# Seven half-size products in the place of eight: an MLP's first matrix product by one level of Strassen's scheme

## The chip, the cores and the metric

One core of a Trainium2 chip runs the kernel. Its engines work side by side: TensorE (PE; PEld is its loading of weights), VectorE (DVE), ScalarE (ACT), GpSimd (POOL) and SyncE (SP), which issues the transfers. The metric is device time of one execution in microseconds (us), as a median of several.

## The reference

The model is four layers deep: two hybrid attention layers, then two more layers, each with an attention mixer, an MLP and a small gated addition. There are 512 tokens and 1024 features. The part that is changed is the MLP of the last two layers:

```
hn = rms(h, g_mlp_pre[i])
y = jnp.square(jax.nn.relu(hn @ w_mlp_in[i])) @ w_mlp_out[i]
h = h + rms(y, g_mlp_post[i])
```

`w_mlp_in` is 1024 x 4096 and `w_mlp_out` is 4096 x 1024, all in float32.

## The kernel before

Everything is kept transposed: features on the 128 partitions, the 512 tokens along the free dimension. A 1024-feature activation is therefore eight tiles of 128 x 512 ("kc").

**Precision.** Each float32 operand is split in two tiles of the type fp32r: `h`, the value cast by ACT, and `l`, the rest, found by a subtraction on DVE or POOL. A product is then three matmuls: `wh` by `xh`, `wh` by `xl`, `wl` by `xh`.

**Weights.** `wload` (L370) brings a chunk of weights in pieces of 128 x 512 (256 KB). For each piece SP issues a transfer into a `wraw` buffer (a ring of four), ACT casts it into a `wh` tile (ring of three, L384), and DVE or POOL in the rotation DVE, POOL, DVE subtracts into a `wl` tile (ring of three, L386). I call that a cut. `proj` (L392) makes the matmuls of one chunk into one PSUM bank.

**MLP.** `mlp` (L1339) goes twice through a half of the 4096 hidden features. For each of the half's 16 chunks `fc` it runs `proj` over the eight activation tiles (24 matmuls of 512 columns), takes the maximum with zero on DVE (L1350), squares on POOL (L1351), casts on ACT (L1354) and subtracts on DVE (L1355); the results `fh`, `fl` stand in a ring of 16. Then, for each of the eight output tiles `oc`, it runs `proj` over the 16 hidden tiles (48 matmuls) and copies or adds the bank to `y`. The squared normalisation factor `r2` is multiplied in behind that, so the first product runs on activations that are scaled by the gain alone.

**Around it.** `tail_layer` (L1391) first calls `post`, which normalises the mixer's output, adds it to `h` and splits `h` into the activation tiles one kc after the other; the order of these DVE instructions is written out by hand. The weights of the first four chunks (AHEAD) are cut before, into `fh`/`fl` tiles. `ple_load` brings a small operand `p` for the gated addition, and from the third `oc` of the second half on the weights of the gate are brought ahead. PSUM has six banks for matmuls here. Otherwise a planner that works from estimated costs fixes each engine's order when the kernel is built; on the chip every engine runs its list strictly in that order.

Of the kernel before, what the change touches and what calls it, by code (L numbers as in the profile page):

```python
# [33 lines left out]
AHEAD = 4  # L34
# [254 lines left out]
class Kern:  # L289
# [178 lines left out]
    def halves(s, T):  # L468
        return [(0, T)] if T <= 512 else [(0, T // 2), (T // 2, T // 2)]
# [862 lines left out]
    def ple_proj(s, weights):  # L1332
        for w in weights:
            (ps, _, _), = s.proj(w, s.pa, [(0, NX)])
            t = s.t512("s", 16)
            s.nc.scalar.activation(t, ps, AF.Copy, scale=0.5)
            s.pp.append(t)

    def mlp(s, l, acts, rstd, fp, w, ahead):  # L1339
        nc = s.nc  # L1340
        ys = []
        acc = s.new_acc()
        r2 = s.tp.tile([P, NT], F32, tag="rstd", bufs=2, name=s.nm("r2"))
# [47 lines left out]
    def tail_layer(s, l, ys, acc):  # L1391

        with ExitStack() as ps:
            s.rings(ps, **RINGT)
            s.pp = []
            pw = s.ple_weights(l, range(0, PLE1))
            with s.tc.tile_pool(name=f"ff{l}", bufs=16) as fp, s.tc.tile_pool(name=f"pe{l}", bufs=1) as pep:

                w, wg = [], []

                def ftiles():
                    return [fp.tile([P, NX], F32R, tag=x, name=s.nm(x)) for x in ("fh", "fl")]
# [4 lines left out]
                s.ple_load(l, lambda: pep.tile([P, NX], F32R, name=s.nm("p")))  # L1407


                ys, acc = s.mlp(l, acts, rstd, fp, w, lambda oc: wg.append(s.wload(s.a[f"wpg{l}"][oc], s.xtiles)))  # L1410
# [433 lines left out]
```

## Time and profile before

| what | us |
|---|---|
| median of 3 runs (2803.01 to 2809.76) | 2805.97 |
| profiled execution | 2807.34 |
| its span, first to last instruction | 2805.6 |
| first MLP, from its steady part to its last matmul | about 1655 to 1989 |
| second MLP | about 2412 to 2745 |

The profiled execution takes 1.74 us more than its span. The two MLPs are nearly a quarter of the span.

### The profile page before, as it was taken

The page shows a single profiled execution, that of the slowest core. Times are in us where ns is not written, and L with a number is a line of the kernel's source. Part 1 is how long each engine was busy: PE and PEld are TensorE (multiplying, and loading weights), DVE is VectorE, ACT ScalarE, POOL GpSimd, SP SyncE. Part 2 cuts the span into 40 slices and gives each one's busy share as a digit, 9 for nine tenths or more (in the row PEclk, how much of TensorE's full clock was granted, in tenths as well). Part 3 has the DMA queues.
Part 4 walks back from the last instruction along what each step waited for, and adds up shares of the span by engine and source line. Part 5 has one row for each costly group of instructions (what it writes and reads, how often), then busy time and mean ns, then how long its engine had stood idle before and what let it go on. Part 6 is the DMA issues. An engine that isn't in the chain of part 4 may idle for free.

```text
span 2805.6 us, 41607 instructions
## 1 busy us (share of the span) xinstructions
PE 2717.9 (97%) x15114; PEld 2330.4 (83%) x15122; DVE 1601.9 (57%) x2977; ACT 1233.1 (44%) x2275; POOL 1134.6 (40%) x1064
## 2 busy tenths in 40 slices
PE   8999999999999999999999999999998899999999
PEld 8999999999889887887777778888776777888887
DVE  5666667644576666545667763133549776622335
ACT  5545444433454444344456642233334665322332
POOL 3455345432334344345555442134316433422341
PEclk9999999999999999999999999999989999999999
DMA  4222232234322223335422223324223202233341
GB/s 147 66 69 77 76 104 80 80 99 137 100 71 74 71 88 94 99 91 181 115 79 82 73 83 95 96 93 126 76 65 90 72 28 73 77 94 94 95 126 58
DMA packets 145518, 252.09 MB, mean 90 GB/s; under 512 B 19552, under 2 KB 30688, under 8 KB 145312
## 3 DMA queue, kind: packets, MB, share of 16 engines
q1 hardware_dynamic: 145312, 249.43, 29.4%
q8 instruction: 119, 1.95, 0.3%
q14 instruction: 87, 0.71, 0.1%
HBM read 215.26 MB, written 6.42 MB: 79 GB/s over the span
## 4 chain that ended last, share of the span: by engine, by line
PE 85%; DVE 8%; ACT 3%; issue 2%; POOL 1%; DMA 1%; SPq 0%; POOLq 0%; DVEq 0%; ACTq 0%
PE mm L363 70%; PE st L363 5%; PE pv L363 5%; PE ssq L419 2%; PE sm L363 1%; DVE zr L702 1%; DVE sm L515 1%; DVE sc L1790 1%; DVE m L1789 1%; DVE wl L386 0%; PE rb L454 0%; DVE sc L1707 0%; DVE h L1295 0%; PE vt L794 0%; DVE Pl L565 0%
## 5 line engine op out<-in xcount | busy, mean ns | idle before, releaser
L384 ACT CAST wh<-wr 128x512 fp32r<-128x512 f32 (+2 forms) x734 | 442.9, 605 | 933.6 <-PE mm L363 781.7
L363 PE MATMUL mm<-xh,wh 128*128 128x264 f32 (+1 forms) x2328 | 793.4, 342 | 21.1 <-ACT xh L1153 7.6
L363 PE MATMUL mm<-xl,wh 128*128 128x264 f32 (+1 forms) x2344 | 796.7, 341 | 1.8 <-DVE xl L1154 1.8
L363 PE MATMUL mm<-xh,wl 128*128 128x264 f32 (+1 forms) x2328 | 788.8, 340 | 0.6 <-DVE wl L386 0.5
L386 POOL TENSOR_TENSOR wl<-wr,wh 128x512 fp32r<-128x512 f32 (+2 forms) x257 | 329.5, 1282 | 794.7 <-ACT wh L384 786.1
L386 DVE TENSOR_TENSOR wl<-wr,wh 128x512 fp32r<-128x512 f32 (+2 forms) x477 | 364.9, 766 | 370.3 <-ACT wh L384 361.8
L363 PEld LDWEIGHTS mm<-xh,wh 128*128 128x128 f32 x2328 | 440.1, 189 | 74.1 <-issue 8.5
L363 PEld LDWEIGHTS mm<-xl,wh 128*128 128x128 f32 x2344 | 444.3, 190 | 52.0 <-DVE xl L1154 3.1
L363 PEld LDWEIGHTS mm<-xh,wl 128*128 128x128 f32 x2328 | 439.5, 189 | 50.3 <-issue 1.2
L565 POOL TENSOR_TENSOR Pl<-P,Ph 128x512 fp32r<-128x512 f32 (+4 forms) x108 | 130.6, 1209 | 185.2 <-ACT P L564 174.2
L363 PE MATMUL mm<-fh,wl 128*128 128x512 f32 x512 | 202.3, 395 | 0.0
L363 PE MATMUL mm<-fl,wh 128*128 128x512 f32 x512 | 202.0, 395 | 0.0
L363 PE MATMUL mm<-fh,wh 128*128 128x512 f32 x512 | 202.0, 395 | 0.0
L564 ACT ACTIVATE Ph<-st 128x512 fp32r<-128x512 f32 (+4 forms) x224 | 122.1, 545 | 142.5 <-PE st L363 84.9
L565 DVE TENSOR_TENSOR Pl<-P,Ph 128x512 fp32r<-128x512 f32 (+4 forms) x108 | 83.7, 775 | 117.7 <-ACT P L564 102.6
L363 PE MATMUL mm<-c,wh 128*128 128x264 f32 (+2 forms) x480 | 128.9, 355 | 10.6 <-ACT q L1724 4.8
L702 DVE RECIPROCAL zr<-zr 128x128 f32<-128x128 f32 (+1 forms) x144 | 123.2, 916 | 4.0 <-ACT zr L711 3.6
L1351 POOL TENSOR_TENSOR ff<-ff 128x512 f32<-128x512 f32 x64 | 81.6, 1274 | 100.2 <-DVE ff L1350 100.0
L564 ACT ACTIVATE P<-st 128x512 f32<-128x512 f32 (+4 forms) x216 | 116.7, 540 | 4.7 <-POOL Pl L565 2.3
L363 PEld LDWEIGHTS mm<-fl,wh 128*128 128x128 f32 x512 | 96.5, 188 | 22.5
L363 PEld LDWEIGHTS mm<-fh,wl 128*128 128x128 f32 x512 | 96.5, 188 | 22.4
L363 PEld LDWEIGHTS mm<-fh,wh 128*128 128x128 f32 x512 | 96.5, 188 | 22.3
(631 smaller groups left out, 5425.2 us busy)
## 6 DMA issues: line engine op xcount, KB each, us to landing
wr<-in_win_dram SPq DMA_DIRECT2D x240, 256.0 KB
wr<-in_wmi_dram SPq DMA_DIRECT2D x128, 256.0 KB
wr<-in_wmo_dram SPq DMA_DIRECT2D x128, 256.0 KB
wr<-in_wbr_dram SPq DMA_DIRECT2D x48, 256.0 KB
wr<-in_wab_dram SPq DMA_DIRECT2D x48, 256.0 KB
wr<-in_wout_dram SPq DMA_DIRECT2D x32, 256.0 KB
wr<-in_wpg_dram SPq DMA_DIRECT2D x32, 256.0 KB
wr<-in_wuq_dram SPq DMA_DIRECT2D x32, 192.0 KB
```

The costliest lines, as they stand in the source:

```text
L363: s.last_mm = s.nc.tensor.matmul(out, l, r, start=start, stop=stop)
L384: nc.scalar.copy(h, raw)
L386: s.weng[s.wn % len(s.weng)].tensor_sub(l, raw, h.bitcast(F32))
L419: s.summed = s.nc.tensor.matmul(ps[:m, b:b + 1], a[:, P * b:P * b + m], s.ones[:, 0:1], start=first and b == 0, stop=last and b == bs[-1])
L515: nc.vector.tensor_tensor_reduce(out=ps[:, col:col + nk], in0=ps[:, col:col + nk], in1=mk, scale=-1.0, scalar=init, op0=OP.add, op1=OP.min ...
L564: nc.scalar.activation(o[:, :col], ps[:, :col], AF.Exp)
L565: s.pl_eng(ui, hn).tensor_sub(pl[:, :col], p[:, :col], ph[:, :col].bitcast(F32))
L702: s.nc.vector.reciprocal(t[:, a:b], t[:, a:b])
L1351: nc.gpsimd.tensor_mul(f, f, f)
L1789: nc.vector.max(m8, score[b][:, :n])
L1790: nc.vector.match_replace(out=score[b][:, :n], in_to_replace=m8, in_values=score[b][:, :n], imm_value=-3e38)
```

## The change

The first product of the MLP is made for pairs of chunks. With the features in halves (kc 0 to 3 and 4 to 7) and the tokens in halves of 256, a pair of 128-feature output chunks is a 2 x 2 block product; Strassen's scheme (in Winograd's form) makes it with seven block products in the place of eight. Four sums of the weights (`S1` to `S4`) and four sums of the activations replace some operands. The activation sums are made once for each layer by `quarters`; the weight sums are made for each pair in `mlp_pair`. The first four chunks of each layer stay as they were, so there are 14 pairs in each layer.

The second product runs in four parts of eight hidden tiles, and the ring of `fh`/`fl` tiles holds one part. `ple_load` moves into the fourth part. Four tiles (`s.spare`, called `e`) are temporaries of `quarters`, then buffers of `mlp_pair`, and at last tiles of `ple_proj`.

```diff
+    def quarters(s, l, acts, sp, e):
...
+        for j in range(KC // 2):
+            x, y, u, v = e
+            for t, kc in ((x, j), (y, KC // 2 + j)):
+                nc.scalar.activation(t, s.h[kc], AF.Copy, scale=s.gcol(f"fpre{l}", kc))
+            nc.vector.tensor_sub(u[:, :H], x[:, H:], x[:, :H])
+            nc.vector.tensor_sub(u[:, H:], y[:, H:], u[:, :H])
+            nc.vector.tensor_sub(v[:, :H], y[:, H:], x[:, H:])
+            nc.vector.tensor_sub(v[:, H:], y[:, :H], u[:, H:])
+            h, lo = (sp.tile([P, 2 * NX], F32R, tag=t, bufs=4, name=s.nm(t)) for t in ("th", "tl"))
+            for i, t in enumerate((u, v)):
+                r = slice(NX * i, NX * i + NX)
+                nc.scalar.copy(h[:, r], t)
+                nc.vector.tensor_sub(lo[:, r], t, h[:, r].bitcast(F32))
...
+    def mlp_pair(s, l, p, q, e, fp, sp):
...
+        def cut(raw, pool, tags, eng):
+            h, lo = (pool.tile([P, NX], F32R, tag=t, bufs=3, name=s.nm(t)) if pool is sp else
+                     pool.tile([P, 4, P], F32R, tag=t, bufs=3, name=s.nm(t)).rearrange("p m n -> p (m n)") for t in tags)
+            nc.scalar.copy(h, raw)
+            eng.tensor_sub(lo, raw, h.bitcast(F32))
+            return h, lo
...
+        a11 = load(2 * p, 0)
+        a21 = load(2 * p + 1, 0, e[2 + odd])
+        a22 = load(2 * p + 1, 4)
+        a12 = load(2 * p, 4)
+        w11 = cut(a11, s.wp, W, V)
+        G.tensor_add(e[0], a21, a22)
+        w12 = cut(a12, s.wp, W, G if odd else V)
+        G.tensor_sub(e[1], e[0], a11)
+        s2 = cut(e[1], sp, S, V)
+        G.tensor_sub(a21, a11, a21)
+        s1 = cut(e[0], sp, S, G)
+        G.tensor_sub(a12, a12, e[1])
+        s3 = cut(a21, sp, S, V)
+        w22 = cut(a22, s.wp, W, G)
+        s4 = cut(a12, sp, S, V)
...
+        prod(b1, 0, w11, q[0], True, True)
+        nc.scalar.copy(t[:, :H], b1[:, :H])
+        prod(b2, 1, w12, q[1], True, False)
+        prod(b2, 0, s2, q[5], False, True)
+        u2 = t[:, H:NX]
+        V.tensor_add(u2, t[:, :H], b2[:, :H])
+        V.tensor_add(g[:, :H], t[:, :H], b2[:, H:])
+        prod(b3, 0, s1, q[4], True, False)
+        prod(b3, 1, s3, q[6], False, True)
...
+        V.tensor_tensor(two(v), u2.unsqueeze(1).to_broadcast([P, 2, H]), two(b3), op=OP.add)
+        V.tensor_add(g[:, 3 * H:], v[:, H:], b3[:, :H])
+        prod(b4, 1, w22, q[3], True, False)
+        prod(b4, 0, s4, q[2], False, True)
+        V.tensor_add(g[:, H:3 * H], v, b4)
+        V.scalar_tensor_tensor(g, g, 0.0, g, op0=OP.max, op1=OP.mult)
...
+        nc.scalar.copy(fh, g)
+        V.tensor_sub(fl, g, fh.bitcast(F32))
...
-        for half in range(2):
+        for part in range(4):
...
+            for p in range(4 * part + len(ff) // 2, 4 * part + 4):
+                ff += s.mlp_pair(l, p, q, s.spare, fp, sp)
             for oc in range(KC):
-                if half == 1 and oc in range(2, 2 + AHEAD):
+                if part == 3 and oc in range(2, 2 + AHEAD):
                     ahead(oc - 2)
-                (ps, _, _), = s.proj(s.wload(s.a[f"wmo{l}"][oc, :, 16 * half:16 * half + 16]), ff, [(0, NX)])
+                (ps, _, _), = s.proj(s.wload(s.a[f"wmo{l}"][oc, :, 8 * part:8 * part + 8]), ff, [(0, NX)])
...
```

Each `prod` is 12 matmuls of 256 columns. `V` is DVE and `G` is POOL.

## Rows read from the trace of the kernel before

**Rows 1.** The page: busy us (share of the span) and instructions of TensorE.
```profile
PE 2717.9 (97%) x15114; PEld 2330.4 (83%) x15122; DVE 1601.9 (57%) x2977; ACT 1233.1 (44%) x2275; POOL 1134.6 (40%) x1064
```

**Rows 2.** Stretches of the first MLP: length, busy us by engine, granted clock, DMA.
```profile
1655.00:1719.00 64.00, 64.00 (x277) 51.72 (x276) 27.63 (x40) 21.84 (x37) 26.61 (x22) 1.00 0.29 91
1719.00:1815.00 96.00, 96.00 (x415) 77.82 (x414) 17.37 (x26) 25.66 (x44) 15.67 (x12) 1.00 0.31 95
1815.00:1909.00 94.00, 94.00 (x407) 75.93 (x405) 35.41 (x54) 29.92 (x51) 35.76 (x29) 1.00 0.29 94
1909.00:1990.00 81.00, 80.63 (x356) 65.64 (x354) 24.82 (x33) 25.37 (x42) 33.07 (x24) 1.00 0.38 120
```

**Rows 3.** The chain that ended last, whole span: start us, us, what.
```profile
566.58 105.49 PE mm L363 x864
...
1620.40 3.40 DMA wr<-in_wmi_dram
...
1655.10 319.36 PE mm L363 x1374
...
2411.96 320.88 PE mm L363 x1386
```

**Rows 4.** DVE in order of time, the MLP's seventh and eighth chunk: start us, us, instruction.
```profile
1670.02 0.69 DVE L1350 TENSOR_SCALAR ff<-mm 128x512 f32<-128x512 f32 x1 [1.08 <-PE mm L363]
1675.60 0.69 DVE L1350 TENSOR_SCALAR ff<-mm 128x512 f32<-128x512 f32 x1 [2.01 <-PE mm L363]
```

**Rows 5.** TensorE in order of time, near the end of the span.
```profile
2795.06 0.39 PE L363 MATMUL mm<-fh,fl 128*128 128x512 f32 x1
2795.29 0.28 PE L363 MATMUL mm<-fh,fh 128*128 128x256 f32 x1
...
2800.92 0.28 PE L363 MATMUL mm<-fh,fl 128*128 128x256 f32 x1
```

**Rows 6.** Groups of instructions by line and shape, 1655 to 1719 us.
```profile
L1351 POOL TENSOR_TENSOR ff<-ff 128x512 f32<-128x512 f32 x13 | 16.4, 1264 | 19.0 <-DVE ff L1350 19.0
L384 ACT CAST wh<-wr 128x512 fp32r<-128x512 f32 x23 | 14.3, 620 | 28.3 <-PE mm L363 22.2 <-issue 6.1
L386 DVE TENSOR_TENSOR wl<-wr,wh 128x512 fp32r<-128x512 f32 x15 | 11.0, 738 | 10.1 <-ACT wh L384 10.1
L386 POOL TENSOR_TENSOR wl<-wr,wh 128x512 fp32r<-128x512 f32 x8 | 10.4, 1296 | 17.8 <-ACT wh L384 17.8
L1355 DVE TENSOR_TENSOR fl<-ff,fh 128x512 fp32r<-128x512 f32 x13 | 9.8, 755 | 13.3 <-ACT fh L1354 13.2
L1350 DVE TENSOR_SCALAR ff<-mm 128x512 f32<-128x512 f32 x12 | 8.3, 689 | 13.6 <-PE mm L363 13.5
```

**Rows 7.** DVE in order of time, in the stretch before the first MLP.
```profile
1629.61 0.74 DVE L1292 SCALAR_TENSOR_TENSOR xh<-xh,gain,rb 128x512 f32<-128x512 f32 x1
1630.26 1.62 DVE L386 TENSOR_TENSOR wl<-wr,wh 128x512 fp32r<-128x512 f32 x1
1631.80 1.78 DVE L1263 SCALAR_TENSOR_TENSOR xl<-h,gain,xh 128x512 fp32r<-128x512 f32 x1
1633.50 0.68 DVE L1295 TENSOR_TENSOR h<-h,xh 128x512 f32<-128x512 f32 x1
...
1644.79 1.62 DVE L1263 SCALAR_TENSOR_TENSOR xl<-h,gain,xh 128x512 fp32r<-128x512 f32 x2
```

**Rows 8.** POOL in order of time, the same stretch.
```profile
1630.03 2.99 POOL L484 TENSOR_TENSOR acc<-acc,sq 128x512 f32<-128x512 f32 x2 [2.10 <-issue]
```

**Rows 9.** The chain's last pieces, on 256-column operands: start us, us, what.
```profile
2801.24 0.39 ACT th L1383
...
2801.65 0.44 DVE th L1384
...
2802.11 0.42 DVE h L1385
```

**Rows 10.** TensorE in order of time: the last matmul of the four prepared chunks.
```profile
1656.33 0.39 PE L363 MATMUL mm<-xh,fl 128*128 128x512 f32 x1
```

More of the change, by code (lines that the diff above doesn't have):

```diff
@@ L1334, in ple_proj @@
             (ps, _, _), = s.proj(w, s.pa, [(0, NX)])
-            t = s.t512("s", 16)
+            t = s.spare.pop(0) if s.spare else s.t512("s", 16)
             s.nc.scalar.activation(t, ps, AF.Copy, scale=0.5)
             s.pp.append(t)
-    def mlp(s, l, acts, rstd, fp, w, ahead):
+    def quarters(s, l, acts, sp, e):
         nc = s.nc
-        ys = []
+        H = NX // 2
+        q = [[] for _ in range(7)]
+        for j in range(KC // 2):
[11 more added lines that the diff above has]
+                nc.vector.tensor_sub(lo[:, r], t, h[:, r].bitcast(F32))
+            for k, (c, r) in enumerate(((j, slice(0, H)), (KC // 2 + j, slice(0, H)), (KC // 2 + j, slice(H, NX)))):
+                q[k].append((acts[c][0][:, r], acts[c][1][:, r]))
+            for k, i in ((4, 0), (5, 1), (6, 2), (3, 3)):
+                r = slice(H * i, H * i + H)
+                q[k].append((h[:, r], lo[:, r]))
+        return q
@@ new lines, in mlp_pair, with load, prod @@
+    def mlp_pair(s, l, p, q, e, fp, sp):
+        nc = s.nc
+        H = NX // 2
+        src = s.a[f"wmi{l}"]
+        s.wn += 1
+        odd = s.wn % 2
+        def load(ch, k0, t=None):
+            t = s.wp.tile([P, 4, P], F32, tag="wraw", bufs=4, name=s.nm("wr")) if t is None else \
+                t.rearrange("p (m n) -> p m n", m=4)
+            nc.sync.dma_start(t, src[ch, :, k0:k0 + 4])
+            return t.rearrange("p m n -> p (m n)")
+        def cut(raw, pool, tags, eng):
[4 more added lines that the diff above has]
+            return h, lo
+        W, S = ("wh", "wl"), ("sh", "sl")
+        V, G = nc.vector, nc.gpsimd
+        a11 = load(2 * p, 0)
[13 more added lines that the diff above has]
+        s4 = cut(a12, sp, S, V)
+        b1, b2, b3, b4 = (s.bank("mm", "mm") for _ in range(4))
+        def prod(ps, c, w, xs, first, last):
+            o = ps[:, H * c:H * c + H]
+            for j, (xh, xl) in enumerate(xs):
+                r = slice(P * j, P * j + P)
+                s.mm(o, w[0][:, r], xh, first and j == 0, False)
+                s.mm(o, w[0][:, r], xl, False, False)
+                s.mm(o, w[1][:, r], xh, False, last and j == 3)
+        t, v = s.tmp("t"), s.tmp("v")[:, :NX]
+        g = sp.tile([P, 2 * NX], F32, tag="g", name=s.nm("g"))
+        prod(b1, 0, w11, q[0], True, True)
[7 more added lines that the diff above has]
+        prod(b3, 1, s3, q[6], False, True)
+        two = lambda x: x.rearrange("p (b c) -> p b c", b=2)
+        V.tensor_tensor(two(v), u2.unsqueeze(1).to_broadcast([P, 2, H]), two(b3), op=OP.add)
[4 more added lines that the diff above has]
+        V.scalar_tensor_tensor(g, g, 0.0, g, op0=OP.max, op1=OP.mult)
+        fh, fl = (fp.tile([P, 2 * NX], F32R, tag=x, name=s.nm(x)) for x in ("fh", "fl"))
+        nc.scalar.copy(fh, g)
+        V.tensor_sub(fl, g, fh.bitcast(F32))
+        return [(fh[:, :NX], fl[:, :NX]), (fh[:, NX:], fl[:, NX:])]
@@ L1342, in mlp @@
+    def mlp(s, l, acts, rstd, fp, sp, w, tiles, ahead):
+        nc = s.nc
         acc = s.new_acc()
@@ L1344, in mlp @@
         nc.gpsimd.tensor_mul(r2[:, :NX], rstd[:, :NX], rstd[:, :NX])
-        for half in range(2):
+        ys = [s.t512("s", 16) for _ in range(KC)]
+        s.spare = [s.t512("s", 16) for _ in range(4)]
+        q = s.quarters(l, acts, sp, s.spare)
+        for part in range(4):
             ff = []
-            for fc in range(16):
-                (ps, _, _), = s.proj(w.pop(0) if w else s.wload(s.a[f"wmi{l}"][16 * half + fc]), acts, [(0, NX)])
+            for fc in range(len(w)):
+                (ps, _, _), = s.proj(w.pop(0), acts, [(0, NX)])
                 f = s.tmp("ff")[:, :NX]
@@ L1351, in mlp @@
                 nc.gpsimd.tensor_mul(f, f, f)
-                fh = fp.tile([P, NX], F32R, tag="fh", name=s.nm("fh"))
-                fl = fp.tile([P, NX], F32R, tag="fl", name=s.nm("fl"))
+                fh, fl = tiles()
                 nc.scalar.copy(fh, f)
@@ L1394, in tail_layer, with halves, get, ahead @@
             s.rings(ps, **RINGT)
-            s.pp = []
+            s.pp, s.spare = [], []
             pw = s.ple_weights(l, range(0, PLE1))
-            with s.tc.tile_pool(name=f"ff{l}", bufs=16) as fp, s.tc.tile_pool(name=f"pe{l}", bufs=1) as pep:
+            with s.tc.tile_pool(name=f"ff{l}", bufs=4) as fp, s.tc.tile_pool(name=f"st{l}", bufs=1) as sp:
                 w, wg = [], []
-                def ftiles():
-                    return [fp.tile([P, NX], F32R, tag=x, name=s.nm(x)) for x in ("fh", "fl")]
+                def halves(pool, tags):
+                    left = []
+                    def get():
+                        if not left:
+                            a, b = (pool.tile([P, 2 * NX], F32R, tag=x, bufs=4, name=s.nm(x)) for x in tags)
+                            left.extend([(a[:, :NX], b[:, :NX]), (a[:, NX:], b[:, NX:])])
+                        return left.pop(0)
+                    return get
+                ftiles, stiles = halves(fp, ("fh", "fl")), halves(sp, ("th", "tl"))
+                def ahead(oc):
+                    if oc == 0:
+                        pt = [x for _ in range(2) for x in stiles()]
+                        s.ple_load(l, lambda: pt.pop(0))
+                    wg.append(s.wload(s.a[f"wpg{l}"][oc], s.xtiles))
                 acts, acc = s.post(ys, acc, f"mpost{l}", f"fpre{l}", pw, lambda: w.extend(
@@ L1406, in tail_layer @@
                 rstd = s.rstd_of(acc, NX, 1024)
[L1407 to L1410 removed]
+                ys, acc = s.mlp(l, acts, rstd, fp, sp, w, ftiles, ahead)
                 pw = s.ple_weights(l, range(PLE1, 4))
```

13 lines of the change are left out of this document (6 added, 7 removed).

## The prediction, made before the changed kernel had run

> **What bounds the kernel now.** I read the page's first table first: TensorE is busy for 97% of the span [rows 1]. That share could hide slack, so I looked at the MLP by stretches: from 1655 to 1990 us TensorE has next to no idle time, while in the two stretches that hold the first product, 158 us together, DVE and POOL each have some 95 us of room [rows 2]. The chain of waits says the same more sharply. One unbroken piece of matmuls is 319.36 us long in the first MLP and 320.88 us in the second [rows 3]. So today a microsecond taken from TensorE there is a microsecond of the kernel, as long as nobody else becomes late.
>
> The pace: the seventh and the eighth chunk are evicted 5.58 us apart [rows 4], and a chunk is 24 matmuls, so a 512-column matmul costs 232.5 ns. I take this and not the chain's 319.36/1374, because a few matmul records may be missing.
>
> **What the products save.** A pair of chunks costs 2 x 5.58 = 11.16 us. After the change it is 7 x 12 = 84 matmuls of 256 columns. What is one worth? The trace has 48 of them: the first starts at 2795.29, the last at 2800.92, which is 5.63/47 = 120 ns each, while the 512-column one just before takes 0.23 us [rows 5]. That stretch is quiet; but 864 matmuls of 264 columns in a loaded stretch take 105.49 us, 122.1 ns each [rows 3], so load hardly costs narrow matmuls anything. I take 120 ns: 10.08 us a pair, 1.08 us saved, 30 us over 28 pairs. Bounds: half of 232.5 (116 ns, 39 us saved) and 120 plus the 5 ns by which 512 columns are slower in the MLP than in the quiet stretch (125 ns, 18 us saved).
>
> The Trainium skill ("TensorE: Matmul & The Clock Gate", Back-to-back issue gap) gives 262 cycles for 256 columns, which at its 2.4 GHz is 109 ns, and 518 cycles, 216 ns, for 512. By that the saving would be 33 us as an estimate; the rows show 120 and 232.5 ns, and they decide.
>
> **What the weight sums cost.** Before, a pair needs four cuts and two evictions. Now it needs seven cuts (ACT 0.62 us each), four sums on POOL, and on POOL also the low parts of s1, w22 and, in every other pair, w12: 6.5 POOL instructions of 1.30 us, 8.4 us [rows 6]. DVE makes 4.5 low parts, five additions from PSUM (three of 256 columns, two of 512, some 2.6 us by 0.42 and 0.69 us [rows 6, 9]) and two instructions over 1024 columns, which no row shows. From 0.42 us for 256 and 0.69 for 512 columns I estimate 1.2 us each. Alone, each of the two engines fits into 10.08 us.
>
> They are not alone. In the stretch before the MLP, DVE's subtraction at 1630.26 takes 1.62 us in the place of 0.68, and the next instruction 1.78 [rows 7], and POOL's two additions, begun at 1630.03, take 2.99 us and not 2.6 [rows 8]. The ends fit a strict turn: DVE finishes at 1631.88 and 1633.58, one POOL instruction apart. The DVE instruction at 1629.61, which takes one operand from PSUM, ran beside POOL at its usual 0.74 us [rows 7]. So a DVE instruction with two SBUF operands and a POOL instruction exclude each other, and one of each costs 1.70 us together (1633.58 - 1631.88). In the MLP as it is, this is rare: the subtractions there average 738 and 755 ns [rows 6].
>
> A pair now has 6.5 POOL instructions and 6.5 such DVE instructions, two of them twice as wide (0.55 us for the other 512 columns, from (0.69 - 0.42)/256 x 512): 6.5 x 1.70 + 2 x 0.55 = 12.15 us, more than TensorE's 10.08. The second product pays back: in its 96 us [rows 2] DVE and POOL are nearly idle. What counts is how much of the sums is done ahead. The rings for `sh`/`sl` and `wh`/`wl` hold three, so about one pair can be. In a part with four pairs TensorE needs 40.3 us, and the last cut must stand 1.44 us before its end, at 38.9. Until then this shared access must carry the rest of the first pair (w22 1.3, s4 0.55, two wide ones at 1.1: 4.0 us), two pairs less the two sums made ahead (24.3 - 2.6), the fourth without its wide ones (10.0), and two cuts for the second product (two thirds on DVE: 0.8 each): 37.3 us. With no gap it just fits. But both engines run in order, behind ACT's casts and ring places that matmuls free; I take nine tenths as used, so 41.4 us and 2.5 us of TensorE waiting. Bounds: none, and 7.7 us at eight tenths.
>
> **End of a part.** The second product now needs its seventh hidden tile after 18 matmuls, 4.2 us. From the last product of a pair that tile takes 0.69 (addition), 1.2, some 1.1 on ACT (from 0.39 and 0.62 us [rows 6, 9]) and 1.2: 4.2 us and the hand-overs. I take 0.5 us of wait; bounds 0 and 1.5.
>
> A full part: -4.32 + 2.5 + 0.5 = -1.3 us; there are six: -7.9 us.
>
> **Opening of the MLP.** The temporaries of `quarters` are the very tiles into which a21 is loaded and the first two weight sums are written. So the first pair's sums can't begin before `quarters` ends. The activations are complete at 1646.4 [rows 7]. DVE then owes the normalisation's 1.1 us and four times (four subtractions over 256 columns, 0.42 us, two over 512, 0.69): 12.2 us. Then the load of a21 (3.40 us in the chain [rows 3]), two sums on POOL (2.6), a cast and a subtraction (1.3), 0.3 for hand-overs: S2's product starts at 1667.3. TensorE's four direct chunks end at 1656.6 [rows 10]; until then it used to make a few matmuls of the next two chunks between them, and w11 and w12 (2.9 us) can take their place. w22 (1.4) fills a little more. So TensorE waits some 9 us. Four products (5.8) and a pair (10.1) end at 1683.1; with 1.5 us of the waits above, 1684.6. Before, the eighth chunk ended at 1675.6 [rows 4]. That is 9.0 us lost in each layer, 18 in both. Bounds: 2 each if half of `quarters` slips in among DVE's earlier work (6 us earlier) and the chain is a microsecond shorter, 17 each if DVE's other work comes first.
>
> **Small parts.** Sixteen more additions of `y` in each layer (0.69 us) read PSUM, so neither POOL nor TensorE waits; if DVE were full they would add 11 us of its time. The weights of the second product are the same bytes in the same pieces. In the fourth part the gate's weights and `p` come in 45 us in the place of 90, four pieces in 5.58 us through four `wraw` buffers, where one load takes 3.40 us [rows 3]: 0.5 us in each layer, 1 in all, up to 4 each. POOL's squares and DVE's maxima of 28 pairs go; they were hidden.
>
> **Sum.** -7.9 + 18 + 1 = +11.1 us on the profiled 2807.34, so 2818.4; that execution is 1.4 us above the median of 2805.97, so 2817, 0.4% slower. A measurement of this kernel tells about 0.2% (5.6 us) from no change.
>
> **Rivals.** (1) *Not slower: the shared access never holds TensorE up.* For: 37.3 us fit before 38.9, and the order may put sums ahead while the second product runs. Against: hardly any room is left. Each full part gives 0.5 - 4.32 = -3.8 us, and 6 x -3.8 + 19 = -3.9: 2802; with an opening of 6 us, 2796. Not slower begins at a use of about 0.92. Chance 0.25: 0.13 within 0.2%, 0.12 faster.
>
> (2) *A short opening.* For: DVE waits for POOL's turns before 1646 [rows 7], gaps an order made from estimates may mean to fill. Against: DVE runs there back to back. At 2 us in each layer, -7.9 + 4 + 1 = -2.9: 2803; without the waits in the parts, 2787. Chance 0.20: 0.13 faster, 0.07 within.
>
> (3) *The shared access sets the pace.* For: 12.15 against 10.08 us a pair, and the turn-taking in [rows 7, 8]. Against: little of it in the MLP so far [rows 6]. At a use of 0.85 TensorE waits 5.0 us in a part: 6 x 1.2 + 19 = +26, 2832; at 0.8, 2848. Chance 0.19, slower. The Trainium skill ("GPSIMD Engine Reference", Key points) has this as a rule: POOL shares its SBUF interfaces with VectorE and contends with DVE instructions that read two SBUF inputs. By that rule the trace agrees, with 1.78 us for a 0.7 us instruction.
>
> (4) *A long opening.* The direct chunks' eight DVE instructions (5.5 us) and POOL's turns come ahead of `quarters`: 8 us more in each layer, 2833. Chance 0.07, slower.
>
> (5) *Narrow matmuls don't save*, at 125 ns: 2817 + 12 = 2829. Against: [rows 5] and the 122.1 ns. Chance 0.03, slower.
>
> **How the numbers follow.** The forecast has 0.26: 0.22 slower, 0.04 within 0.2%; its own range is 2809 to 2826. Faster: 0.12 + 0.13 = 0.25. Same: 0.13 + 0.07 + 0.04 = 0.24. Slower: 0.22 + 0.19 + 0.07 + 0.03 = 0.51. The range from 2788 to 2840 takes in rivals 1 and 2 down to their low ends, and rival 3 to a use of 0.83.
>
> **What would show it.** Right: matmuls of 256 columns at 120 ns; DVE subtractions and POOL instructions in the pairs well above 0.69 and 1.30 us; TensorE idle for some 9 us before S2's first product, with the load of a21 behind `quarters`, and for 2 to 3 us in each four pairs, waiting for `sl`, `wl` or POOL's sums; second products at 5.58 us for 24 matmuls. Wrong: pairs following each other at 10.1 us to the end of a part (rival 1), or at 12 and more from the second on (rival 3); no gap in the opening (rival 2); a first product of the fourth pair that waits for a transfer; or a granted clock below 1.00 inside the MLP, which I have not priced.

## The result and the profile after

The changed kernel takes 2854.57 us (median of four, 2852.99 to 2858.71) against 2806.83 for the kernel before (2803.01 to 2809.76): a ratio of 1.0178, 95% interval 1.0166 to 1.019. It is 48 us slower, where 11 were forecast, and lies outside the stated range of 2788 to 2840. The profiled execution has a span of 2852.8 us, 47.2 more than before.

The page's first line answers to [rows 1]:

```profile
PE 2707.2 (95%) x16122; PEld 2371.0 (83%) x16130; DVE 1841.4 (65%) x3193; ACT 1301.6 (46%) x2391; POOL 1316.6 (46%) x1152
```

TensorE has 10.7 us less work than before, DVE 239 us and POOL 182 us more, and TensorE's share of the span falls. To see where, I cut both MLPs at the same events: from the first of the norm's 40 small matmuls (line 419) to the last eviction of each part (the instruction that copies or adds an output bank to `y`; the expectations count the parts from 0). Before, a part is a quarter of the MLP: the first ends eight chunks' pitch behind the eighth chunk [rows 4], 1675.60 + 8 x 5.58 - 1609.89 = 110.3 us, a middle one takes 16 x 5.58 = 89.2, and the last is what remains.

| us, first / second MLP | forecast, each | before | after | change |
|---|---|---|---|---|
| opening and part 1 | +9.0 | 110.3 / 109.7 | 129.0 / 128.1 | +18.7 / +18.4 |
| part 2 | -1.3 | 89.2 / 88.6 | 89.0 / 89.5 | -0.2 / +0.9 |
| part 3 | -1.3 | 89.2 / 88.6 | 88.5 / 90.9 | -0.7 / +2.3 |
| part 4 | -0.8 | 90.3 / 90.1 | 95.1 / 95.9 | +4.8 / +5.8 |

That is +50 us in the MLPs. The rest of the kernel has the same code, yet its order came out differently (+3.8 us up to the first norm, -8.1 between the MLPs, +1.7 behind them): together some 2.7 us less, which I don't explain.

**The stretches** of the first MLP answer to [rows 2] (length, busy us of PE, PEld, DVE, ACT, POOL, granted clock, DMA):

```profile
1650.00:1680.00 30.00, 14.95 (x67) 11.62 (x66) 23.96 (x36) 13.72 (x25) 12.98 (x11) 0.74 0.10 32
...
1702.00:1745.00 43.00, 43.00 (x198) 35.16 (x197) 12.35 (x14) 15.76 (x28) 14.24 (x11) 1.00 0.30 93
1745.00:1794.00 49.00, 45.33 (x346) 43.06 (x345) 42.60 (x46) 19.65 (x33) 35.39 (x21) 1.00 0.31 97
...
1833.00:1883.00 50.00, 47.03 (x358) 44.69 (x357) 42.40 (x46) 20.89 (x35) 37.65 (x23) 1.00 0.31 95
```

Three things are to be seen: TensorE half idle in the opening, at a lower clock; no idle time in a second product (1702 to 1745); and 3.0 to 3.7 us of it in each four pairs, with DVE busy for 42.6 of 49 us and POOL for 35.4. Much of these two shares is waiting inside an instruction, as the rows of the pairs below show.

In the second MLP the granted clock is below 1.00 inside the pairs too. These are the pairs of its third and fourth part, and TensorE behind a wait in the third:

```profile
2603.00:2652.00 49.00, 44.96 (x348) 43.79 (x348) 41.71 (x45) 19.33 (x34) 36.78 (x22) 0.97 0.29 92
2693.70:2740.00 46.30, 42.77 (x327) 42.09 (x327) 39.44 (x43) 19.35 (x34) 35.05 (x21) 0.93 0.26 81
```

```profile
2623.50 0.47 PE L363 MATMUL mm<-xh,sl 128*128 128x256 f32 x1 [1.94 <-DVE sl L1383]
2623.77 0.42 PE L363 MATMUL mm<-xh,sh 128*128 128x256 f32 x1
2623.98 0.42 PE L363 MATMUL mm<-xl,sh 128*128 128x256 f32 x1
```

Five such runs of 14 to 16 matmuls, 0.21 us apart and not 0.12, stand behind waits of 1.3 to 2.1 us in the pairs: one in the first MLP (fourth part), four in the second (one each in the second and third part, two in the fourth). They cost some 1.4 us each, 7 us in all. Not every wait of that length has one: the 2.14 us before 1775.25 and 1863.76 have none.

**The opening in TensorE's time.** TensorE in order of time, around its one long gap:

```profile
1662.17 1.02 PE L454 MATMUL rb<-rstd,ones 128*128 128x512 f32 x2
1677.73 0.58 PE L363 MATMUL mm<-th,sh 128*128 128x256 f32 x1 [14.54 <-ACT sh L1382]
...
1681.20 0.41 PE L363 MATMUL mm<-th,wl 128*128 128x256 f32 x1
1681.41 0.36 PE L363 MATMUL mm<-xh,wh 128*128 128x256 f32 x1
1681.61 0.28 PE L363 MATMUL mm<-xl,wh 128*128 128x256 f32 x1
1681.72 0.28 PE L363 MATMUL mm<-xh,wl 128*128 128x256 f32 x1
```

S2's product starts after 14.54 us of nothing, 64.1 us after the norm's sums begin (63.9 in the second MLP, with 14.52 us); the forecast had it at 57.4 and the wait at 9. Behind the gap most of the narrow matmuls stand 0.21 to 0.22 us apart, from 1681.6 on 0.12. So the first seventeen ran at the lower of the clock's two levels (1.2 GHz; the granted clock is 0.54 from 1677 to 1682 and 1.00 in the 4 us behind): 3.88 us in the place of 17 x 0.12, 1.8 us lost.

What TensorE waited for is in the chain of waits:

```profile
1670.10 0.60 DVE fl L1454
1670.70 0.61 DVE tl L1357
1671.38 2.92 DMA s<-in_wmi_dram
1674.44 1.25 POOL s L1393
1675.78 1.27 POOL s L1395
1677.06 0.63 ACT sh L1382
1677.73 13.34 PE mm L363 x95
```

The last subtraction of `quarters` (L1357), the load of a21 into the tile that this sets free, two sums, a cast. That is the predicted chain, and from the load on it takes 6.35 us (7.6 forecast). The error is ahead of it: `quarters` ends at 1671.3, 57.7 us after the norm's sums begin, and not 49.8 us after them (1659.7 by the times of the kernel before). DVE in order of time, in the stretch that answers to [rows 7]:

```profile
1645.45 0.41 DVE L1350 TENSOR_TENSOR s<-s,s 128x256 f32<-128x256 f32 x1
1645.78 1.51 DVE L1351 TENSOR_TENSOR s<-s,s 128x256 f32<-128x256 f32 x1
1647.22 0.68 DVE L1295 TENSOR_TENSOR h<-h,xh 128x512 f32<-128x512 f32 x1
...
1654.32 0.74 DVE L1263 SCALAR_TENSOR_TENSOR xl<-h,gain,xh 128x512 fp32r<-128x512 f32 x1
```

And the stretch around it, with the columns of the stretches above:

```profile
1636.00:1656.00 20.00, 19.21 (x92) 15.32 (x91) 20.00 (x27) 11.17 (x19) 9.73 (x7) 0.96 0.00 0
```

DVE has no free moment. The subtractions of `quarters` (L1349 to L1357) stand between the activation tiles, and one of 256 columns that meets POOL takes 1.51 us and not 0.41. So the last activation tile is ready at 1655.06, 41.4 us after the norm's sums begin, where it was 36.5 (1646.4 - 1609.9), and `quarters` goes on among the maxima and subtractions of the direct chunks until 1671.3.

**A pair.** DVE in the second part: the squared maximum (L1430) and the last subtraction (L1433) of a pair are the two instructions over 1024 columns.

```profile
1754.64 2.31 DVE L1430 SCALAR_TENSOR_TENSOR g<-g 128x1024 f32<-128x1024 f32 x1
1756.87 1.78 DVE L1383 TENSOR_TENSOR wl<-wr,wh 128x512 fp32r<-128x512 f32 x1
1758.58 2.31 DVE L1433 TENSOR_TENSOR fl<-g,fh 128x1024 fp32r<-128x1024 f32 x1
1760.81 0.41 DVE L1420 TENSOR_TENSOR t<-t,mm 128x256 f32<-128x256 f32 x1
...
1767.26 2.31 DVE L1430 SCALAR_TENSOR_TENSOR g<-g 128x1024 f32<-128x1024 f32 x1
...
1780.38 2.32 DVE L1430 SCALAR_TENSOR_TENSOR g<-g 128x1024 f32<-128x1024 f32 x1
...
1788.84 1.23 DVE L1430 SCALAR_TENSOR_TENSOR g<-g 128x1024 f32<-128x1024 f32 x1
```

What is uncontended at 1.23 us takes 2.31, and 512 columns take 1.78, while the addition that reads PSUM (L1420) keeps its 0.41. The squared maxima of three pairs stand 12.6 and 13.1 us apart, the last 8.5 us behind the third, when POOL makes one low part of a weight (at 1785.9) and no more sums. The shared access was forecast at 12.15 us a pair.

**The end of the MLP.** DVE's last eviction in the first MLP, before, with its wait for the last matmul, which ends at 1988.85:

```profile
1988.88 0.69 DVE L1367 TENSOR_TENSOR s<-s,mm 128x512 f32<-128x512 f32 x1 [4.71 <-PE mm L363]
```

And after, where the last matmul ends at 2011.62:

```profile
2009.26 1.78 DVE L386 TENSOR_TENSOR tl<-wr,th 128x512 fp32r<-128x512 f32 x1
2013.13 2.13 DVE L386 TENSOR_TENSOR tl<-wr,th 128x512 fp32r<-128x512 f32 x2 [2.09 <-ACT th L384]
2015.18 0.68 DVE L1466 TENSOR_TENSOR s<-s,mm 128x512 f32<-128x512 f32 x1
```

The eviction is 3.6 us late (2.1 in the second MLP) and waits for no matmul: two cuts of the gate's weights stand before it in DVE's list, and the second waits for ACT. I had priced late transfers here, and not the order of DVE's list.

### The profile page after: what moved, and what is told of

It is laid out like the page before. It is cut to its first block, busy times and chain, and to the rows that moved or that the text cites. A ratio compares the mean times of both kernels' runs of the same rounds, so it can differ in the third digit from the quotient of the medians.

```text
span 2852.8 us, 44225 instructions
## 1 busy us (share of the span) xinstructions
PE 2707.2 (95%) x16122; PEld 2371.0 (83%) x16130; DVE 1841.4 (65%) x3193; ACT 1301.6 (46%) x2391; POOL 1316.6 (46%) x1152
## 4 chain that ended last, share of the span: by engine, by line
PE 76%; DVE 13%; issue 3%; ACT 3%; DMA 2%; POOL 2%; SPq 0%; POOLq 0%; DVEq 0%; ACTq 0%
PE mm L363 61%; PE st L363 5%; PE pv L363 5%; PE ssq L419 2%; PE sm L363 1%; DVE zr L702 1%; DMA wr<-in_wmi_dram 1%; DVE sl L1383 1%; DVE g L1430 1%; DVE fl L1433 1%; DVE sm L515 1%; DVE sc L1906 1%; DVE wl L1383 1%; DVE m L1905 0%; DVE wl L386 0%
## 5 line engine op out<-in xcount | busy, mean ns | idle before, releaser
L384 ACT CAST wh<-wr 128x512 fp32r<-128x512 f32 (+2 forms) x622 | 373.5, 602 | 772.7 <-PE mm L363 631.1
L363 PE MATMUL mm<-xh,wh 128*128 128x264 f32 (+2 forms) x2104 | 683.4, 326 | 22.8 <-ACT xh L1153 7.8
L363 PE MATMUL mm<-xl,wh 128*128 128x264 f32 (+2 forms) x2120 | 687.5, 326 | 1.8 <-DVE xl L1154 1.8
L363 PE MATMUL mm<-xh,wl 128*128 128x264 f32 (+2 forms) x2104 | 678.9, 324 | 0.6 <-DVE wl L386 0.5
L386 POOL TENSOR_TENSOR wl<-wr,wh 128x512 fp32r<-128x512 f32 (+2 forms) x221 | 289.1, 1308 | 672.4 <-ACT wh L384 658.4
L363 PEld LDWEIGHTS mm<-xh,wh 128*128 128x128 f32 x2104 | 401.9, 192 | 56.4 <-issue 9.9
L386 DVE TENSOR_TENSOR wl<-wr,wh 128x512 fp32r<-128x512 f32 (+2 forms) x401 | 315.2, 787 | 206.0 <-ACT wh L384 195.2
L363 PEld LDWEIGHTS mm<-xl,wh 128*128 128x128 f32 x2120 | 406.0, 192 | 33.1 <-DVE xl L1154 3.0
L363 PEld LDWEIGHTS mm<-xh,wl 128*128 128x128 f32 x2104 | 400.9, 191 | 31.0 <-issue 1.2
L565 DVE TENSOR_TENSOR Pl<-P,Ph 128x512 fp32r<-128x512 f32 (+4 forms) x108 | 87.4, 809 | 121.5 <-ACT P L564 109.9
L363 PE MATMUL mm<-th,sh 128*128 128x256 f32 x336 | 96.1, 286 | 29.1 <-ACT sh L1382 29.1
```

The source lines that it names most:

```text
L363: s.last_mm = s.nc.tensor.matmul(out, l, r, start=start, stop=stop)
L384: nc.scalar.copy(h, raw)
L386: s.weng[s.wn % len(s.weng)].tensor_sub(l, raw, h.bitcast(F32))
L565: s.pl_eng(ui, hn).tensor_sub(pl[:, :col], p[:, :col], ph[:, :col].bitcast(F32))
```

## Experiments

Theory: the loss is the opening, where DVE has more to do than I counted before the first sums can be made, and in the pairs the turns of DVE and POOL take back what the products save. Rivals: the tiles that `quarters` shares are to blame, not the work; the second product in four parts costs the time by itself; the order of DVE's work decides. Each ratio is against runs of the kernel before on the same chip. All twelve, in the segments of the table above (us; middle is the mean of parts 2 and 3 of both MLPs). Segments are those of the profiled execution, which can lie off the run's median: 9.6 us below it in no sums, 10.8 above it in balance, within 5 in the others.

| run | median | ratio (95%) | opening and part 1 | middle | part 4 |
|---|---|---|---|---|---|
| before | 2806.8 | | 110.3 / 109.7 | 88.9 | 90.3 / 90.1 |
| the change | 2854.6 | 1.0178 (1.0166 to 1.019) | 129.0 / 128.1 | 89.5 | 95.1 / 95.9 |
| own tiles | 2850.1 | 1.0149 (1.0127 to 1.017) | 127.8 / 128.3 | 89.2 | 95.4 / 95.5 |
| eight direct | 2829.1 | 1.0076 (1.0056 to 1.0095) | 115.4 / 119.2 | 90.5 | 96.6 / 94.9 |
| parts only | 2812.0 | 1.0018 (1.0008 to 1.0027) | 110.8 / 110.2 | 88.9 | 94.2 / 93.3 |
| no sums | 2815.2 | 1.0021 (1.0007 to 1.0035) | 125.5 / 125.7 | 84.4 | 89.0 / 87.8 |
| balance | 2823.4 | 1.0065 (1.004 to 1.0089) | 130.3 / 127.9 | 85.5 | 90.1 / 87.4 |
| eight direct, later | 2826.7 | 1.0079 (1.0054 to 1.0103) | 115.2 / 116.3 | 89.0 | 95.9 / 94.3 |
| balance and that | 2796.0 | 0.9967 (0.9954 to 0.998) | 115.9 / 119.3 | 85.2 | 88.8 / 87.3 |
| and the fourth part | 2792.5 | 0.9948 (0.9931 to 0.9965) | 115.4 / 116.6 | 85.5 | 88.6 / 86.2 |
| and quarters held | 2783.8 | 0.9914 (0.9899 to 0.9929) | 110.8 / 113.0 | 84.9 | 88.8 / 85.6 |
| gate loaded behind | 2800.1 | 0.9973 (0.9958 to 0.9987) | 115.2 / 116.2 | 85.7 | 87.3 / 87.5 |
| change, held | 2859.5 | 1.0184 (1.0169 to 1.0199) | 131.5 / 131.4 | 89.0 | 95.9 / 96.1 |
| change, held less | 2852.4 | 1.0152 (1.0129 to 1.0175) | 128.5 / 129.3 | 88.5 | 95.4 / 96.6 |

### Own tiles

```diff
-            x, y, u, v = e
+            x, y = e[0], s.tmp("qy")[:, :NX]
+            gt = sp.tile([P, 2 * NX], F32, tag="g", name=s.nm("qg"))
+            u, v = gt[:, :NX], gt[:, NX:]
...
-        q = s.quarters(l, acts, sp, s.spare)
+        q = s.quarters(l, acts, sp, [sp.tile([P, NX], F32, name=s.nm("qx"))])
```

> Kernel after, but quarters works in tiles of its own, so that the load of a21 and the first weight sums need not wait for its end. Theory 'chain' (the opening is long because a21's load, two POOL sums and a cut stand in a row behind quarters): S2's first product starts about 6 us earlier in each layer, 2854.6 - 12 = 2843 us. Rival 'DVE is full' (the opening is long because DVE and POOL's turns in it are more than there is time for): S2's first product waits for the activation sums all the same, less than 2 us gained in each layer, 2851 to 2855 us.

2850.1: 4.5 us gained and not 12, and only 1 us of it in the two openings. The sums of the first pair do run early now, in the opening, but each takes a turn from DVE. POOL in order of time:

```profile
1639.37 1.75 POOL L1397 TENSOR_TENSOR s<-s,wr 128x512 f32<-128x512 f32 x1
1641.07 1.74 POOL L1399 TENSOR_TENSOR s<-wr,s 128x512 f32<-128x512 f32 x1
1642.78 1.74 POOL L484 TENSOR_TENSOR acc<-acc,sq 128x512 f32<-128x512 f32 x1
```

One instruction every 1.70 or 1.71 us, as long as DVE's with two SBUF operands stand against it; the last activation tile is ready at 1658.6 and not at 1655.1. The first product on sums now starts 50.5 us after the norm's sums begin and not 64.1, but the later ones wait for `quarters`, which ends 70.3 us after them; from 1645.0 to 1682.4 the chain that ended last runs through DVE's list, but for some 4 us on ACT. So the shared tiles are not what makes the opening long: DVE's list, with POOL's turns in it, is.

### Eight direct chunks

```diff
-            for fc in range(len(w)):
-                (ps, _, _), = s.proj(w.pop(0), acts, [(0, NX)])
+            for fc in range(8 if part == 0 else 0):
+                (ps, _, _), = s.proj(w.pop(0) if w else s.wload(s.a[f"wmi{l}"][fc]), acts, [(0, NX)])
```

> Kernel after, but all eight chunks of the first part are direct ones, so 24 pairs and not 28, and quarters and the first pair have 22 us more of direct matmuls beside them. Theory 'opening' (18.6 us a layer are lost before the first part's last pair): about 17 us a layer come back, less 2 us for the pairs not made, 2854.6 - 2 x 16 = 2822 us, TensorE without the 14.5 us gap. Rival 'pairs' (the time is lost in every pair alike, 1.7 us in each): four pairs fewer, 2854.6 - 7 = 2848 us.

2829.1, 25 us better (32 by the theory of the opening, 7 by its rival) though 4 of the 28 pairs, with their forecast 1.08 us each, are given up. With the whole first part done directly, TensorE has no wait for `quarters` in it; its longest there are for low parts of weights (1.02 and 2.79 us). So the opening is the larger part of the loss; 5 to 10 us of it stay.

### Parts only

```diff
-        q = s.quarters(l, acts, sp, s.spare)
...
-            for fc in range(len(w)):
-                (ps, _, _), = s.proj(w.pop(0), acts, [(0, NX)])
+            for fc in range(8):
+                (ps, _, _), = s.proj(w.pop(0) if w else s.wload(s.a[f"wmi{l}"][8 * part + fc]), acts, [(0, NX)])
```

> Second product in four parts with the rings, the moved load of p and the tiles of the kernel after, but every chunk by the direct first product: no Strassen. Theory 'fourth part by itself' (the gate's weights, p and POOL's products come in 45 us in place of 90): about 4 to 6 us lost at the end of each layer, and the ends of the other parts hidden: 2807 + 10 = 2817 us. Rival 'it needs the pairs' (the fourth part is slow because the pairs leave POOL late): 2805 to 2809 us.

2812.0, between the theory's 2817 and the rival's 2805 to 2809. The first three parts cost nothing; the last is 3 to 4 us longer, with no pair in it. DVE at its end, where the last matmul ends at 1991.98:

```profile
1993.34 2.12 DVE L386 TENSOR_TENSOR tl<-wr,th 128x512 fp32r<-128x512 f32 x2 [2.02 <-ACT th L384]
1995.37 0.68 DVE L1465 TENSOR_TENSOR s<-s,mm 128x512 f32<-128x512 f32 x1
```

The late eviction (3.4 us here, 1.4 in the second MLP) belongs to the division in four parts, with what moved into the fourth, and not to the products.

### No sums

```diff
-        G.tensor_add(e[0], a21, a22)
-        G.tensor_sub(e[1], e[0], a11)
-        s2 = cut(e[1], sp, S, V)
-        G.tensor_sub(a21, a11, a21)
-        s1 = cut(e[0], sp, S, G)
-        G.tensor_sub(a12, a12, e[1])
+        s2 = cut(a22, sp, S, V)
+        s1 = cut(a21, sp, S, G)
```

> Kernel after without the four weight sums on POOL: s1 to s3 are cut from a21, a22 and a11 - a part of the input - and s4 from a12, so the first product leaves out the sums; everything else runs. Theory 'shared access' (a POOL instruction and a DVE instruction with two SBUF operands exclude each other, 12.6 us a pair): the access carries about 7.5 us a pair, TensorE's idle time in the full parts (3 to 4.5 us each) goes, and the opening is 2.6 us shorter: 2854.6 - 22 - 5 = 2828 us, with the 1024-column DVE instructions mostly at 1.2 us in place of 2.3. Rival 'rings and transfers' (TensorE waits for ring places and loads): less than 8 us gained.

This kernel leaves out the four weight sums. 2815.2, 39 us less. The stretch of four pairs:

```profile
1736.00:1784.00 48.00, 48.00 (x358) 45.81 (x358) 31.73 (x48) 21.50 (x35) 11.40 (x9) 1.00 0.33 102
```

TensorE never waits, a middle part takes 84.4 us, and that is what the products save when nothing holds them up: 88.9 - 84.4 = 4.5 us in four pairs, 4.32 forecast.

### Balance

```diff
-        w12 = cut(a12, s.wp, W, G if odd else V)
+        w12 = cut(a12, s.wp, W, V)
-        s1 = cut(e[0], sp, S, G)
+        s1 = cut(e[0], sp, S, V)
-        w22 = cut(a22, s.wp, W, G)
+        w22 = cut(a22, s.wp, W, V)
-        V.scalar_tensor_tensor(g, g, 0.0, g, op0=OP.max, op1=OP.mult)
+        nc.scalar.activation(g, g, AF.Relu)
+        nc.scalar.activation(g, g, AF.Square)
```

> Kernel after, but the three low parts that POOL makes (s1, w22, w12) go to DVE, and maximum and square of a pair (one 1024-column DVE instruction with two SBUF operands) go to ACT as Relu and Square. POOL keeps the four sums. Theory 'shared access': a pair then takes 4 x 1.70 + 3 x 0.55 + 0.55 = 9.0 us of it in place of 12.2 and fits into TensorE's 10.1; a full part goes from 89 to about 85 us as in the run without sums, 6 x -4 and a little in the opening: 2854.6 - 25 = 2830 us. Rival 'the sums come too late in order' (POOL's chain of four sums and the ring places hold TensorE up, not the access): full parts stay at 88 us or more, 2846 to 2856 us.

2823.4, 31 us less, with all four sums in place: POOL keeps only those, DVE takes the low parts, ACT the maximum and the square.

```profile
1749.00:1797.00 48.00, 46.98 (x353) 44.67 (x352) 37.79 (x49) 27.36 (x41) 18.68 (x13) 1.00 0.29 97
```

POOL's 35.4 us of 49 have become 18.7 of 48, ACT has 27.4, and TensorE's idle time in the stretch falls from 3.7 to 1.0 us; no run of slow matmuls is left in the pairs of parts 2 to 4. A low part on DVE costs 0.6 us of the shared access, a POOL instruction with DVE's next to it 1.70.

### Eight direct chunks with quarters later

The edit of eight direct chunks, and:

```diff
-        q = s.quarters(l, acts, sp, s.spare)
+        with s.tc.issue_after(s.spreads.ins):
+            q = s.quarters(l, acts, sp, s.spare)
```

> Run e2 (eight direct chunks in the first part), and quarters is held back until the MLP's normalisation factor is made, so that its DVE work doesn't come between the activation tiles. Theory 'DVE is full before the activations are ready': the first part, 115.4 and 119.2 us in e2 against 110.3 in the kernel before, falls to about 111.5: 2829 - 4 - 7 = 2818 us. Rival 'the work only moves' (what quarters owes then holds up the first pairs of the second part): 2826 to 2832 us.

2826.7, 2.4 us from eight direct chunks alone, no more than the noise. The hold did not act: DVE's first subtraction of `quarters` (L1349) stands at 1640.17 among the activations, as it does without it (1639.87). So this run says nothing of a later `quarters`.

### Both, and the fourth part

Balance with the edit just above:

> Runs e5 and e6 together. If both effects are what the theories say and add up: 2818 - 24 = 2794 us, faster than the kernel before. Rivals: if the shared access is not the cause, 2815 or more.

2796.0, 0.33% faster than before. That it is near the expected 2794 is luck: balance had given 31 us for the 24 reckoned, and the hold 2 for 11. Then also the gate's weights spread over the last part and the scaling of `y` moved from POOL to DVE:

```diff
-                if part == 3 and oc in range(2, 2 + AHEAD):
-                    ahead(oc - 2)
+                if part == 3 and oc % 2:
+                    ahead(oc // 2)
...
-                    (nc.vector if oc == KC - 1 else nc.gpsimd).tensor_mul(y, y, r2[:, :NX])
+                    nc.vector.tensor_mul(y, y, r2[:, :NX])
```

> Run e7, and in the fourth part the gate's weights are brought at every other output tile in place of four in a row, and the product of y with its factor is made by DVE in place of POOL. Theory 'the fourth part crowds POOL and the transfers': the 4 to 6 us that the fourth part takes over the others come back in each layer, 2794 - 8 = 2786 us. Rival 'it is the load of p and of the gate itself': 2790 to 2796 us.

2792.5, not clear of the run before (the intervals overlap): the last parts gave 0.2 and 1.1 us. In the first MLP the eviction is still 2.6 us late (3.1 before this edit), in the second on time (0.9).

### And quarters held

On top of that version, `quarters` is held by its data: a copy of the gain that needs `rstd`.

```diff
-        with s.tc.issue_after(s.spreads.ins):
-            q = s.quarters(l, acts, sp, s.spare)
+        o = GAIN[f"fpre{l}"]
+        g2 = s.tp.tile([P, KC], F32, tag="g2", name=s.nm("g2"))
+        nc.vector.scalar_tensor_tensor(g2, rstd[:, :KC], 0.0, s.gain[:, o:o + KC], op0=OP.mult, op1=OP.add)
+        q = s.quarters(l, acts, sp, s.spare, g2)
...
-                nc.scalar.activation(t, s.h[kc], AF.Copy, scale=s.gcol(f"fpre{l}", kc))
+                nc.scalar.activation(t, s.h[kc], AF.Copy, scale=g2[:, kc:kc + 1])
```

> The best version so far (eight direct chunks, balanced pairs, gate weights spread out; 2792.5 us), and in it the two copies that begin each of the four rounds of quarters are scaled by a gain that DVE copies only after rstd is made, so that quarters really cannot start before the activations are complete. If the 5 to 6 us still lost in part 0 of each layer come from DVE making quarters between the activation tiles, part 0 falls from 115.4 and 116.6 us to about 111 and the time by 4 in each layer, to about 2784. Rival: the work only moves into DVE's time with the direct chunks, whose hidden tiles then come late: part 0 stays at 115 or more and the time at 2792 or above.

2783.8, the expected number, and the openings are 4.6 and 3.6 us shorter, for the 4 expected in each. The stretch that was half idle in the change:

```profile
1650.00:1680.00 30.00, 28.90 (x132) 23.12 (x131) 24.48 (x40) 16.78 (x29) 13.43 (x10) 1.00 0.15 44
```

Opening and part 1 take 110.8 and 113.0 us, within 3.3 us of the kernel before. Both MLPs are shorter than before, 369 us each for 379 and 377: 18 of the 19.6 us between the spans of the two profiled executions. The medians on this run's chip are 25 us apart; where the rest of that lies no profile shows.

### The gate loaded behind the MLP

```diff
-                    wg.append(s.wload(s.a[f"wpg{l}"][oc], s.xtiles))
...
+                wg.extend(s.wload(s.a[f"wpg{l}"][oc], s.xtiles) for oc in range(AHEAD))
                 pw = s.ple_weights(l, range(PLE1, 4))
```

> The best version so far (2792.5 us), but the gate's four chunks of weights are loaded and cut behind the MLP and no longer during the fourth part; p is still loaded there. If these loads are what keeps the fourth part 2 to 4 us above the others (88.6 and 86.2 against about 85), it falls to 85 to 86 us; what the gate then waits for its weights shows behind the MLP and makes the kernel as a whole slower by some microseconds. Rival: the fourth part is long because of the squares and the scaling that its evictions add, or because of p; then it stays at 86 to 88.6.

2800.1, and inconclusive: the planner still cut the gate's weights (the first row, with `xh`) before the last eviction, and other weights too (the second row).

```profile
1983.90 0.85 DVE L386 TENSOR_TENSOR xl<-wr,xh 128x512 fp32r<-128x512 f32 x1 [2.25 <-ACT xh L384]
1984.68 0.69 DVE L386 TENSOR_TENSOR wl<-wr,wh 128x512 fp32r<-128x512 f32 x1
1985.29 0.68 DVE L1468 TENSOR_TENSOR s<-s,mm 128x512 f32<-128x512 f32 x1
```

The last eviction is 2.0 and 2.8 us late. A place later in the program did not keep the work out of the part. But the lateness accounts for the part: less it, the fourth part takes 84.7 to 86.5 us in all five versions with balanced pairs, and the middle parts 84.9 to 85.7.

### The change with quarters held

The hold by `rstd` alone, on the changed kernel with its four direct chunks:

> The changed kernel (2854.6 us) with nothing but the hold of quarters behind rstd, four direct chunks as in the change. If the opening is long because quarters' instructions stand among the activations and delay them, the activations come some 8 us earlier, quarters runs in one piece behind them and S2's first product starts 3 to 6 us earlier against the start of the norm's sums; opening and part 0 fall from 129 and 128 us to 123 to 126, the time to 2843 to 2849. Rival: the amount of DVE's work ahead of the first sums decides and not its order: the opening stays at 128 or more, 2854 or above.

2859.5: the number is the rival's. The last activation is ready at 1650.6, 36.5 us after the norm's sums begin, as before the change; so the order was repaired. But `quarters` now starts late. Its first and last instructions on DVE:

```profile
1662.53 0.43 DVE L1349 TENSOR_TENSOR s<-s 128x256 f32<-128x256 f32 x1 [0.19 <-ACT s L1348]
...
1674.30 1.29 DVE L1357 TENSOR_TENSOR tl<-s,th 128x512 fp32r<-128x512 f32 x2 [0.23 <-ACT th L1356]
```

Nearly in one piece it takes 13.1 us (12.2 forecast), and S2's product starts 67.9 us after the sums begin.

### Held less

The gain copy now needs only the last activation tile, so that `quarters` starts where the prediction put it:

```diff
-        nc.vector.scalar_tensor_tensor(g2, rstd[:, :KC], 0.0, s.gain[:, o:o + KC], op0=OP.mult, op1=OP.add)
+        nc.vector.scalar_tensor_tensor(g2, acts[KC - 1][1][:, :KC].bitcast(F32), 0.0, s.gain[:, o:o + KC], op0=OP.mult, op1=OP.add)
```

> As the run before (the changed kernel with quarters held), but the gain copy that starts quarters waits only for the eighth and last activation tile, not for rstd: quarters begins where the prediction put it, right behind the activations, some 36 to 37 us after the norm's sums begin and not 48. By the prediction's chain (13 us of quarters, 6.4 us of load, sums and cut) S2's first product starts 57 to 60 us after those sums begin (64.0 in the changed kernel, 67.9 with the hold behind rstd), opening and part 0 take 121 to 125 us and the kernel 2840 to 2847. Rival: the work for the four direct chunks and POOL's turns come between in any order, S2 starts at 62 or later, and opening and part 0 stay at 127 or more, the time at 2851 or above.

2852.4: the rival's number again. `quarters` begins 37.1 us after the sums begin and ends 58.2 us after them, 21 us later. DVE in order of time:

```profile
1652.29 0.42 DVE L1349 TENSOR_TENSOR s<-s 128x256 f32<-128x256 f32 x1 [0.79 <-ACT s L1348]
...
1661.67 0.68 DVE L1453 TENSOR_SCALAR ff<-mm 128x512 f32<-128x512 f32 x1
1662.27 0.41 DVE L1350 TENSOR_TENSOR s<-s,s 128x256 f32<-128x256 f32 x1
1662.60 1.52 DVE L1457 TENSOR_TENSOR fl<-ff,fh 128x512 fp32r<-128x512 f32 x1
...
1672.05 1.29 DVE L1357 TENSOR_TENSOR tl<-s,th 128x512 fp32r<-128x512 f32 x2 [0.23 <-ACT th L1356]
```

From start to start a 256-column instruction stands for 0.34 us and one of 512 for 0.60, so the 24 of `quarters` come to 10.2 us; the eight of the direct chunks to 4.8; four instructions that wait a turn of POOL, which squares the maxima and `rstd`, lose 0.85 each, 3.4; `rstd` and a weight's low part 1.3. That is 19.7 of the 21.1 us; the rest is short waits for ACT. S2's product starts 64.5 us after the sums begin; in the changed kernel, with another order of the same work, 64.1. So what set the opening is the amount of DVE's work that stands ahead of the first sums. That all of it must stand there is not shown: no run put `quarters` ahead of the direct chunks' eight instructions. At the 13.1 us that it took nearly in one piece, it would then end some 8 us earlier (an estimate: 21.1 - 13.1).

## Why the prediction was wrong

- **Right: the direction, and what bounds each part.** Narrow matmuls stand 0.12 us apart at the full clock, second products keep their pace, without the 0.5 us of wait that was reckoned for the end of a part, and the products save 4.5 us in four pairs where nothing holds them up (no sums).
- **Right: the shared access in the pairs.** 12.15 us a pair were forecast, 12.6 and 13.1 are seen. The wait was a little small: 2.9 to 4.0 us of idle TensorE in the four middle parts, for 2.5. A full part came out at -0.7 to +2.3 us for -1.3; with four middle parts that is +2.3 in all for -5.2. No sums and balance show the cause from both sides: less on POOL, next to no wait.
- **The step that failed: "Opening of the MLP".** The sum let DVE owe 13.3 us behind the activations; it owed 21 (held less). The direct chunks' eight instructions, `rstd` and POOL's turns were in the prediction, but as rival 4, at 0.07, not in the sum. That puts S2's product 6.7 us late of the 9.7 that the opening missed; the lower clock behind the gap adds 1.8, and the remaining 1.2 are further waits in that part. In both layers: +37.1 us for +18. That `quarters` ran among the activations and not behind them made no difference to S2's start (64.1 and 64.5 us).
- **A term put at nothing: the clock inside the MLP.** The prediction named a granted clock below 1.00 there as a sign of being wrong, and had not priced it. It came: five runs of matmuls at half pace behind waits in the pairs, some 7 us in all. Of the +0.9 and +2.3 us of the second MLP's middle parts, 1.4 each are this.
- **Also mis-sized: the fourth part.** -0.8 each forecast, +4.8 and +5.8 measured. 3.6 and 2.1 us of these are the last eviction behind cuts of the gate's weights, and parts only shows it without a pair. What is left beyond that is TensorE's waits, as in the middle parts, and the lower clock behind them (1.3 and 2.8 us). That moving these cuts would give the time back was shown only in small: where the spread loads put the eviction on time, in one MLP, the part was 1.1 us shorter; in the other run they did not leave the part.
- **Rivals.** Rival 1 (no waiting) fell, and balance shows that it was a matter of which engine does what. Rival 2 (a short opening) fell by 16 us a layer; its low end, 2787, comes to 2788 by its own terms. Rival 3 came halfway: the access set the pace inside the pairs, 12.6 to 13.1 us, and second products paid it back. Rival 4 is what happened in the opening. Its 17 us a layer for it are 1.4 to 1.7 short of the measured ones.

The Trainium skill ("GPSIMD Engine Reference", Key points) says that POOL contends with DVE instructions that have two SBUF inputs. The traces agree, with 1.23 us that become 2.31, and with 0.41 us for an instruction that reads PSUM in the same stretch.

## What to carry to other kernels

Where a cheaper product buys its saving with preparation on other engines, count for each of them everything that its list holds between the event that starts the preparation and the first product that needs it, not the preparation alone. Begin with work that needs none of it, long enough to cover the rest: here eight direct chunks instead of four turned 129 and 128 us into 115 and 119. And give an engine pair that excludes each other as few couples as can be: with POOL left the sums alone in the pairs, ACT taking maximum and square, eight direct chunks, the gate's weights spread out and `quarters` held behind the activations, the same scheme is 0.86% faster than the kernel before (0.71 to 1.01%).

## What the runs showed that I had not expected

- The turns hold for short instructions too. A DVE subtraction of 256 columns takes 0.41 us alone and 1.51 behind a POOL instruction, so a small instruction can cost nearly what a wide one does.
- In the opening of own tiles, POOL keeps to one instruction every 1.70 or 1.71 us; alone, one takes it 1.30. DVE gets one instruction with two SBUF operands into each such turn, where it could start one every 0.60 us.
- After 14.54 us without a matmul, TensorE's next seventeen run at half speed (0.21 us in the place of 0.12) though they follow each other without a wait. So do 14 to 16 matmuls behind some waits of 1.3 to 2.1 us in the pairs: such a wait can cost 1.4 us more than itself.
